# Input products of two FFNs, two feature tiles at a time, as seven half-size products

## The chip, the cores and the metric

One core of a Trainium2 chip runs the whole program. The metric is the time of one execution on the device in microseconds (us), as the median of several runs. Engines carry the profile's names: PE multiplies matrices, PEld is its weight load, DVE, ACT and POOL compute on vectors, SP issues most transfers; POOL and ACT can issue transfers too.

## The reference

Two streams of 256 tokens each, latent `x` and context `xc`, pass two layers of width 1024. A layer is FFN, token mixer, FFN; the context stream needs no second mixer output and no last FFN. What the change touches are the FFNs:

```python
def _swiglu(h, w1, w3, w2):
    return (jax.nn.silu(h @ w1) * (h @ w3)) @ w2
for l in range(DEPTH):
    x  = x  + mx[2] * 0.5 * _swiglu(_modulate(x,  norm_gain[l, 0], mx[0], mx[1]), ffn1_w1[l], ffn1_w3[l], ffn1_w2[l])
    xc = xc + mc[2] * 0.5 * _swiglu(_modulate(xc, norm_gain[l, 0], mc[0], mc[1]), ffn1_w1[l], ffn1_w3[l], ffn1_w2[l])
    ...
    x  = x  + mx[8] * 0.5 * _swiglu(_modulate(x,  norm_gain[l, 2], mx[6], mx[7]), ffn2_w1[l], ffn2_w3[l], ffn2_w2[l])
```

`h` is 512 tokens by 1024 and `w1`, `w3` are 1024 by 2816 (22 feature tiles of 128). All is float32. The vectors `mx`, `mc` come from the conditioning vector by a product with `ada_w` (nine vectors of 1024 per layer and stream).

## The kernel before, in words

Features lie on the 128 partitions, the 512 tokens on the columns: latent tokens are columns 0 to 255 (`HX`), context tokens 256 to 511 (`HC`). Every float32 product is made of three PE matmuls: an operand is cut into a high part and a rest, and `mm3` (lines 211 to 213) adds rest by high, high by rest and high by high.

- **Weights.** `unit` (line 187) loads 128x1024 weights into a buffer `raw` (four buffers, SP), ACT casts it to `whi` (line 201), DVE subtracts to get `wlo` (line 202); four buffers of each.
- **FFN** (`ffn`). The first two feature tiles are made as soon as the normed chunks `h` come (the start phase, 256 columns at a time). Each further tile takes two units, for `w1` and `w3`, and 48 matmuls of 512 columns: `silu` on ACT, the gate product `gg` on DVE (line 463), and the cut into `g`. The 22 tiles go in groups (`FF_GROUPS`); after each group `out_phase` multiplies its tiles by `w2` for the eight output chunks and adds them to `x` (line 405).
- **Conditioning.** `ada` computes those vectors on DVE: per chunk one load into `araw` (two buffers) and one 128x1024 multiply-and-sum `junk` for each stream (line 276), called a dot below. A call of `hook(n)` issues about 2n dots, after a tile (`HOOK[0]`) or an output chunk (`HOOK[1]`).
- **Order.** PE runs in the order in which the code is written; for the other engines a scheduler sets a fixed order when the program is built. Each engine executes its own in order.

Four FFNs run: layer 0's first (about 20 to 385 us), layer 0's second (936 to 1290), layer 1's first (1300 to 1650) and layer 1's second, on latent tokens alone (2020 to 2215).

## Time and profile before

| | |
|---|---|
| time of the runs | 2222.62 us median of 3 (2222.49 to 2224.86) |
| span of the profiled execution | 2221.8 us |
| PE busy | 2205.7 us (99%), 12165 matmuls |
| weight load PEld busy | 1876.2 us (84%) |
| DVE, ACT, POOL busy | 1451.5 (65%), 944.7 (43%), 95.2 us (4%) |
| moved by DMA | 312.74 MB, mean 141 GB/s |

The span reaches from the first to the last instruction; the median run is 0.8 us longer than it. A busy time is the time in which at least one instruction of that engine was in flight, so pipelined matmuls can fill it without running at their best rate.

### The profile page before, as it was taken

Reading aid. Unit: us, or ns where it says so; the run is one execution under the profiler, and the core shown is the slowest. Engines: PE = TensorE matmul, PEld = TensorE weight load, DVE = VectorE, ACT = ScalarE, POOL = GpSimd, SP = SyncE. Lnnn points to the kernel's source line nnn. Section 1 sums busy time; section 2 is a strip of 40 time slices with the busy share of each in tenths; the row PEclk is TensorE's granted clock in tenths of the full one; section 3 lists DMA queues with packets and bytes.
Section 4 is the critical chain, followed back from the end, with each engine's and each line's share of the span. In section 5 each row is a group of like instructions: output and inputs, shape, how many; then the busy total and the mean of one; then the engine's idle time right before and its main releaser. Section 6 shows DMA issues by size and latency. Waiting matters only on the chain.

```text
span 2221.8 us, 32917 instructions
## 1 busy us (share of the span) xinstructions
PE 2205.7 (99%) x12165; PEld 1876.2 (84%) x12165; DVE 1451.5 (65%) x3452; ACT 944.7 (43%) x2519; POOL 95.2 (4%) x126
## 2 busy tenths in 40 slices
...
GB/s 326 189 217 175 217 185 169 98 88 67 56 80 97 83 58 98 121 186 211 179 215 279 200 76 98 102 89 101 92 127 104 87 114 107 160 137 167 182 181 114
DMA packets 89330, 312.74 MB, mean 141 GB/s; under 512 B 10320, under 2 KB 11216, under 8 KB 89168
## 3 DMA queue, kind: packets, MB, share of 16 engines
...
## 4 chain that ended last, share of the span: by engine, by line
PE 88%; issue 9%; DVE 1%; ACT 1%; DMA 0%; POOL 0%; POOLq 0%; DVEq 0%; SPq 0%; ACTq 0%
PE mm L211 21%; PE mm L212 20%; PE mm L213 20%; PE s L212 6%; PE s L211 6%; PE s L213 6%; PE o L206 2%; PE s L206 2%; PE t L206 2%; PE t L774 1%; PE mm L206 1%; PE t L551 0%; PE s L838 0%; PE s L840 0%; PE t L789 0%
## 5 line engine op out<-in xcount | busy, mean ns | idle before, releaser
L201 ACT CAST whi<-raw 128x256 fp32r<-128x256 f32 (+2 forms) x1446 | 536.7, 433 | 561.7 <-issue 272.1
L202 DVE TENSOR_TENSOR wlo<-raw,whi 128x256 fp32r<-128x256 f32 (+1 forms) x1438 | 587.2, 455 | 269.8 <-ACT whi L201 266.2
L211 PE MATMUL mm<-h,wlo 128*128 128x512 f32 (+1 forms) x1432 | 515.0, 360 | 0.0
L213 PE MATMUL mm<-h,whi 128*128 128x512 f32 (+1 forms) x1432 | 506.0, 353 | 0.0
L212 PE MATMUL mm<-h,whi 128*128 128x512 f32 (+1 forms) x1432 | 505.8, 353 | 0.0
L211 PEld LDWEIGHTS mm<-h,wlo 128*128 128x128 f32 x1432 | 270.7, 189 | 44.8 <-issue 9.4
L213 PEld LDWEIGHTS mm<-h,whi 128*128 128x128 f32 x1432 | 270.6, 189 | 37.8
L212 PEld LDWEIGHTS mm<-h,whi 128*128 128x128 f32 x1432 | 271.0, 189 | 34.8 <-issue 0.2
L276 DVE SCALAR_TENSOR_TENSOR junk<-araw,cond 128x1024 bf16<-128x1024 f32 x224 | 271.3, 1220 | 24.0 <-DMA araw<-in_ada 23.5
L211 PE MATMUL mm<-g,wlo 128*128 128x512 f32 (+1 forms) x767 | 267.4, 349 | 0.0
L212 PE MATMUL mm<-g,whi 128*128 128x512 f32 (+1 forms) x767 | 266.5, 347 | 0.0
L213 PE MATMUL mm<-g,whi 128*128 128x512 f32 (+1 forms) x767 | 266.5, 347 | 0.0
L211 PE MATMUL s<-h,wlo 128*128 128x512 f32 (+1 forms) x688 | 246.9, 359 | 0.0
L212 PE MATMUL s<-h,whi 128*128 128x512 f32 (+1 forms) x688 | 246.9, 359 | 0.0
L213 PE MATMUL s<-h,whi 128*128 128x512 f32 (+1 forms) x688 | 246.9, 359 | 0.0
L405 DVE SCALAR_TENSOR_TENSOR x<-mm,mods,x 128x256 f32<-128x256 f32 x192 | 86.0, 479 | 116.8 <-PE mm L213 116.6
L211 PEld LDWEIGHTS mm<-g,wlo 128*128 128x128 f32 x767 | 145.3, 189 | 18.3
L212 PEld LDWEIGHTS mm<-g,whi 128*128 128x128 f32 x767 | 145.3, 189 | 18.1
L213 PEld LDWEIGHTS mm<-g,whi 128*128 128x128 f32 x767 | 145.3, 189 | 18.1
L461 ACT ACTIVATE silu<-mm 128x512 f32<-128x512 f32 (+1 forms) x88 | 47.9, 544 | 242.5 <-PE mm L213 242.5
L463 DVE TENSOR_TENSOR gg<-silu,s 128x512 f32<-128x512 f32 (+1 forms) x87 | 53.9, 619 | 147.9 <-PE s L213 132.2
L211 PEld LDWEIGHTS s<-h,wlo 128*128 128x128 f32 x688 | 130.3, 189 | 19.2
...
## 6 DMA issues: line engine op xcount, KB each, us to landing
raw<-in_w SPq DMA_DIRECT2D x170, 512.0 KB, 3.9
araw<-in_ada SPq DMA_DIRECT2D x128, 512.0 KB, 3.7
raw<-in_win SPq DMA_DIRECT2D x90, 512.0 KB, 3.3
...
raw<-in_w2a SPq DMA_DIRECT2D x32, 512.0 KB, 3.9
raw<-in_wbr SPq DMA_DIRECT2D x24, 512.0 KB, 3.4
raw<-in_ada SPq DMA_DIRECT2D x16, 512.0 KB, 9.4
raw<-in_wv SPq DMA_DIRECT2D x16, 512.0 KB, 3.6
```

Of the source, the lines that this page charges most:

```text
L201: nc.scalar.copy(hi[:, c], raw[:, c])
L202: eng.tensor_tensor(out=lo[:, c], in0=raw[:, c], in1=hi[:, c].bitcast(F32), op=ALU.subtract)
L206: self.nc.tensor.matmul(out, lhsT=lhsT, rhs=rhs, start=start, stop=stop)
L211: nc.tensor.matmul(out, lhsT=sl, rhs=mh, start=start, stop=False)
L212: nc.tensor.matmul(out, lhsT=sh, rhs=ml, start=False, stop=False)
L213: nc.tensor.matmul(out, lhsT=sh, rhs=mh, start=False, stop=stop)
L276: self.nc.vector.scalar_tensor_tensor(out=junk, in0=raw, scalar=1.0, in1=cond[s], op0=ALU.mult, op1=ALU.mult, accum_out=self.mods[l][:, s, ...
L405: nc.vector.scalar_tensor_tensor(out=self.xT[c][:, hc], in0=ps[:, hc], scalar=self.mods[l][:, s, gm, c:c + 1], in1=self.xT[c][:, hc], op0= ...
L461: nc.scalar.activation(t[:, cols], pa[:, cols], AF.Silu)
L463: nc.vector.tensor_tensor(out=gg[:, cols], in0=t[:, cols], in1=pb[:, cols], op=ALU.mult)
L774: nc.tensor.transpose(pt[:, b * 128:(b + 1) * 128], P[:, b * 128:(b + 1) * 128], self.ident)
```

## The change

For layer 0's second and layer 1's first FFN, all tiles but the first two are taken two at a time. The two tiles, the two halves of the 1024 inputs and the two token streams make a 2 by 2 block product, and seven block products (`product`: 24 matmuls of 256 columns) replace eight. `W[p, 0]` to `W[p, 3]` are the four weight blocks of pair p, from a copy of the weights in that layout; in PE's order the products of a pair take: W1 with b21; W0+W2+W3 with n2; W2+W3 with n1; W0+W2 with n3; the next pair's W0 with b11 (`begin`); W3 with n4; W0+W1+W2+W3 with b22. Results add up in the banks q1, q2, q3 and are put together by ACT and DVE. W2+W3 and W0+W2 are formed by a second, accumulating transfer that POOL issues into the loaded buffer; the other sums are DVE additions. `token_forms` makes n1 to n4 from a float32 copy (`stash`) of the normed inputs, once per FFN.

Besides: the groups become 8, 8 and 6 tiles; the dots of three vectors of layer 1 move into layer 0's first FFN (paced by 3.2 and 1.5), two vectors into layer 0's second and four into layer 1's first, there only in output phases; `cond` and the probability tiles `P` share two wide buffers.

```diff
-FF_GROUPS = ((0, 8), (8, 15), (15, 22))
+FF_GROUPS = ((0, 8), (8, 16), (16, 22))
...
+STRASSEN = ((0, 1), (1, 0))
...
-HOOK = (2.2, 0.9)
+PACE = ((3.2, 1.5), (0.0, 1.0), (0.0, 1.0))
...
         out = []
         for s in range(2):
-            t = self.qkv.tile([128, 1024], F32, tag="pair", name="cond")
+            t = self.wide("cond").rearrange("p a b -> p (a b)")
             queue.dma_start(t, self.a["cvec"][s].to_broadcast([128, 1024]))
             nc.scalar.activation(t, t, AF.Silu)
             out.append(t)
...
-    def start_norm(self, l, j, acc, s, cols, tail):
+    def start_norm(self, l, j, acc, s, cols, tail, stash=False):
         if s == 0:
             self.hn = [self.pair("h", pool=self.hp) for _ in range(KD)]
             self.hready = [0, 0]
+            self.stash = [self.pair("stash", F32) for _ in range(KD // 2)] if stash else None
 
         def apply(R):
             def one(k):
                 self.modulate(self.hn[k], self.xT[k], R, self.gs[l][:, s, j, k:k + 1],
-                              self.mods[l][:, s, 3 * j, k:k + 1], cols)
+                              self.mods[l][:, s, 3 * j, k:k + 1], cols,
+                              self.stash[k // 2][:, k % 2, cols] if stash else None)
                 self.hready[s] = k + 1
                 if k + 1 < KD:
                     self.at(self.clock["pe"] + STEP, lambda: one(k + 1))
...
         return [self.a["w13"][l, i, f, j] for f in range(2) for j in range(2)]
+
+    def token_forms(self, l, j):
+        nc = self.nc
+        M = self.mods[l]
+        X, C = M[:, 0, 3 * j, :], M[:, 1, 3 * j, :]
+        dd = self.small(8, "dshift", 1)
+        nc.vector.tensor_tensor(out=dd[:, 0:4], in0=C[:, 0:4], in1=X[:, 0:4], op=ALU.subtract)
+        nc.vector.tensor_tensor(out=dd[:, 4:8], in0=C[:, 4:8], in1=C[:, 0:4], op=ALU.subtract)
+        n2, n3, n4 = ([self.pair("tf") for _ in range(2)] for _ in range(3))
+        add = nc.vector.scalar_tensor_tensor
+        at = lambda k, cols: self.stash[k // 2][:, k % 2, cols]
+
+        def cut(out, q, cols, sign):
+            src = self.stash[q][:, :, cols]
+            hi, lo = (out[:, i, :].rearrange("p (k t) -> p k t", k=2) for i in range(2))
+            nc.scalar.activation(hi, src, AF.Copy, scale=sign)
+            add(out=lo, in0=src, scalar=sign, in1=hi.bitcast(F32), op0=ALU.mult, op1=ALU.subtract)
+
+        for q in range(2):
+            for k in (2 * q, 2 * q + 1):
+                add(out=at(k, HX), in0=at(k, HC), scalar=dd[:, k:k + 1], in1=at(k, HX), op0=ALU.add, op1=ALU.subtract)
+                add(out=at(k, HC), in0=at(k + 4, HC), scalar=dd[:, 4 + k:5 + k], in1=at(k, HC),
+                    op0=ALU.add, op1=ALU.subtract)
+                hi, lo = self.hn[k][:, 0, HC], self.hn[k][:, 1, HC]
+                nc.scalar.activation(hi, at(k, HX), AF.Copy, scale=-1.0)
+                add(out=lo, in0=at(k, HX), scalar=-1.0, in1=hi.bitcast(F32), op0=ALU.mult, op1=ALU.subtract)
+            cut(n3[q], q, HC, 1.0)
+            for k in (2 * q, 2 * q + 1):
+                add(out=at(k, HX), in0=at(k, HX), scalar=C[:, k + 4:k + 5], in1=at(k + 4, HC),
+                    op0=ALU.subtract, op1=ALU.subtract)
+            cut(n2[q], q, HX, 1.0)
+            for k in (2 * q, 2 * q + 1):
+                add(out=at(k, HX), in0=at(k, HX), scalar=X[:, k + 4:k + 5], in1=at(k + 4, HX),
+                    op0=ALU.add, op1=ALU.add)
+            cut(n4[q], q, HX, -1.0)
...
+        return {"b11": plain(0, HX), "b21": plain(4, HX), "b22": plain(4, HC), "n1": plain(0, HC),
+                "n2": form(n2), "n3": form(n3), "n4": form(n4)}
+
+    def cut_weight(self, raw):
+        nc = self.nc
+        hi, lo = (self.wp.tile([128, 1024], F32R, tag=g, name=g) for g in ("whi", "wlo"))
+        nc.scalar.copy(hi, raw)
+        nc.vector.tensor_tensor(out=lo, in0=raw, in1=hi.bitcast(F32), op=ALU.subtract)
+        return hi, lo
+
+    def block(self, src, plus=None):
+        raw = self.rawp.tile([128, 1024], F32, tag="raw", name="raw")
+        self.nc.sync.dma_start(raw, src)
+        if plus is not None:
+            self.nc.gpsimd.dma_start(raw, plus, accum_op=ALU.add)
+        return raw
+
+    def product(self, out, w, acts, start, stop):
+        hi, lo = w
+        for j in range(2):
+            o = out[:, j * SEQ:(j + 1) * SEQ]
+            c = 0.0
+            for k, (mh, ml) in enumerate(acts):
+                ws = slice(j * 512 + k * 128, j * 512 + (k + 1) * 128)
+                c += self.mm3(o, hi[:, ws], lo[:, ws], mh, ml, start and j + k == 0, k == 3, skip_group_check=True)
+            self.tick(c)
+
+    def ff_pairs(self, l, i, pairs, B):
+
+
+        nc, W = self.nc, self.a["w13p"][STRASSEN.index((l, i))]
+        add = nc.vector.tensor_tensor
+        begun = {}
+
+        def begin(p):
+            r0 = self.block(W[p, 0])
+            q1 = self.mm_bank()
+            self.product(q1, self.cut_weight(r0), B["b11"], True, False)
+            s1 = self.tmp("s1")
+            nc.scalar.copy(s1, q1)
+            begun[p] = r0, q1, s1
+
+        out = []
+        for p in pairs:
+            if p not in begun:
+                begin(p)
+            r0, q1, s1 = begun.pop(p)
+            g1, g2 = (self.pair("g") for _ in range(2))
+            r1 = self.block(W[p, 1])
+            q2, q3 = self.s_bank(), self.s_bank()
+            self.product(q2, self.cut_weight(r1), B["b21"], True, True)
+            add(out=s1, in0=s1, in1=q2, op=ALU.add)
+            self.gated(s1, g1, HX)
+            n = self.block(W[p, 2], W[p, 3])
+            wn = self.cut_weight(n)
+            add(out=r0, in0=r0, in1=n, op=ALU.add)
+            self.product(q1, self.cut_weight(r0), B["n2"], False, False)
+            sv = self.tmp("sv")
+            nc.scalar.copy(sv, q1)
+            self.product(q3, wn, B["n1"], True, False)
+            r3 = self.block(W[p, 0], W[p, 2])
+            self.product(q1, self.cut_weight(r3), B["n3"], False, False)
+            sw = self.tmp("sw")
+            nc.scalar.copy(sw, q1)
+            nc.vector.scalar_tensor_tensor(out=sw, in0=sw, scalar=-1.0, in1=q3, op0=ALU.mult, op1=ALU.subtract)
+            self.gated(sw, g2, HC)
+            if p + 1 < NFF // 2:
+                begin(p + 1)
+            r4 = self.block(W[p, 3])
+            self.product(q1, self.cut_weight(r4), B["n4"], False, True)
+            su = self.tmp("su")
+            nc.scalar.activation(su, q1, AF.Copy, scale=-1.0)
+            self.gated(su, g2, HX)
+            add(out=r1, in0=r1, in1=r0, op=ALU.add)
+            self.product(q3, self.cut_weight(r1), B["b22"], False, True)
+            add(out=sv, in0=sv, in1=q3, op=ALU.add)
+            self.gated(sv, g1, HC)
+            yield [g1, g2]
+
+    def gated(self, f, gt, cols):
+        nc = self.nc
+        u, v = f[:, 0:SEQ], f[:, SEQ:T]
+        nc.scalar.activation(u, u, AF.Silu)
+        nc.vector.tensor_tensor(out=u, in0=u, in1=v, op=ALU.mult)
+        hi, lo = gt[:, 0, cols], gt[:, 1, cols]
+        nc.scalar.copy(hi, u)
+        nc.vector.tensor_tensor(out=lo, in0=u, in1=hi.bitcast(F32), op=ALU.subtract)
 
     def ffn(self, l, i, halves, first, acc, after, pre, begun=None, each=None):
         nc, a = self.nc, self.a
...
                                       k == 0, k == KD - 1)
                     self.tick(c)
             start = [self.ff_evac(banks[2 * f], banks[2 * f + 1], cols) for f in range(2)]
-            self.hook(3)
+            if (l, i) in STRASSEN:
+                pairs = self.ff_pairs(l, i, range(1, NFF // 2), self.token_forms(l, 2 * i))
         else:
             start = begun
         h = self.hn
         for gi, (f0, f1) in enumerate(FF_GROUPS):
             gts = start
             start = []
+            if (l, i) in STRASSEN:
+                while len(gts) < f1 - f0:
+                    gts += next(pairs)
+                    self.hook(self.pace[0])
             for f in range(f0 + len(gts), f1):
                 with self.tc.issue_after(self.last_act) if gi == 0 and f < HOLD and begun is None else nullcontext():
                     wa = self.unit(a["w13"][l, i, f, 0])
                 self.run(self.gemm(pa, wa, h, cols))
                 self.run(self.gemm(pb, wb, h, cols))
                 gts.append(self.ff_evac(pa, pb, cols))
-                self.hook(HOOK[0])
+                self.hook(self.pace[0])
             ng = f1 - f0
-            w2 = a["w2a"][l, i] if gi == 0 else a["w2b"][l, i, gi - 1]
+            w2 = a["w2c"][l, i] if gi == 2 else a["w2a"][l, i, gi]
             end = gi == len(FF_GROUPS) - 1
             self.out_phase(lambda c: self.unit(w2[c], ng * 128), gts, l, gm, halves,
                            acc if end else None, after if end else None, pre if end else None, each if end else None)
             if k + 3 < KD:
                 load(k + 3)
         cond = self.cond(nc.sync)
-        self.adaq = self.ada(0, range(2, NMOD), cond)
+        self.adaq = itertools.chain(self.ada(0, range(2, NMOD), cond), self.ada(1, range(3), cond))
+        self.pace = PACE[0]
...
-            P = [self.tmp("P"), self.tmp("P")]
+            PP = self.wide("P")
+            P = [PP[:, 0, :], PP[:, 1, :]]
...
             acc2 = self.tmp("acc")
             first, pre = self.first_units(self.ff_units(l, 1))
             self.mixer(l, SEQ if last else T, nxt, spills[l], acc2,
-                       lambda *v: self.start_norm(l, 2, acc2, *v), pre)
+                       lambda *v: self.start_norm(l, 2, acc2, *v, stash=not last), pre)
             if not last:
-                self.adaq = self.ada(l + 1, range(NMOD), self.cond(nc.scalar))
+                self.adaq = self.ada(l + 1, range(3, 5), self.cond(nc.scalar))
+                self.pace = PACE[1]
             acc = self.tmp("acc")
             nxt, pre = (None, None) if last else self.first_units(self.ff_units(l + 1, 0))
             if last:
                 self.ffn(l, 1, halves, first, acc, lambda s, hc, tail: self.finish(acc, tail), lambda i: None,
                          each=self.turn_out)
             else:
-                self.ffn(l, 1, halves, first, acc, lambda *v: self.start_norm(l + 1, 0, acc, *v), pre)
+                self.ffn(l, 1, halves, first, acc, lambda *v: self.start_norm(l + 1, 0, acc, *v, stash=True), pre)
                 first = nxt
+                self.run(self.adaq)
+                self.adaq = self.ada(l + 1, range(5, NMOD), self.cond(nc.scalar))
+                self.pace = PACE[2]
```

Where instructions move, two places matter. The first is one feature tile in the middle of layer 0's first FFN on DVE, between two gate products (`gg`). Before:

```order
L463 TENSOR_TENSOR gg<-silu,s 128x512
L276 SCALAR_TENSOR_TENSOR junk,mods_106<-araw,cond 128x1024
L379 TENSOR_TENSOR g<-gg,g 128x512
L276 SCALAR_TENSOR_TENSOR junk,mods_106<-araw,cond 128x1024 x2
L202 TENSOR_TENSOR wlo<-raw,whi 128x256
L276 SCALAR_TENSOR_TENSOR junk,mods_106<-araw,cond 128x1024
L202 TENSOR_TENSOR wlo<-raw,whi 128x256 x7
L463 TENSOR_TENSOR gg<-silu,s 128x512
```

The same tile on DVE with the change:

```order
L470 TENSOR_TENSOR gg<-silu,s 128x512
L281 SCALAR_TENSOR_TENSOR junk,mods_106<-araw,cond 128x1024
L384 TENSOR_TENSOR g<-gg,g 128x512
L281 SCALAR_TENSOR_TENSOR junk,mods_106<-araw,cond 128x1024 x2
L207 TENSOR_TENSOR wlo<-raw,whi 128x256
L281 SCALAR_TENSOR_TENSOR junk,mods_106<-araw,cond 128x1024
L207 TENSOR_TENSOR wlo<-raw,whi 128x256 x3
L281 SCALAR_TENSOR_TENSOR junk,mods_106<-araw,cond 128x1024
L207 TENSOR_TENSOR wlo<-raw,whi 128x256
L281 SCALAR_TENSOR_TENSOR junk,mods_106<-araw,cond 128x1024
L207 TENSOR_TENSOR wlo<-raw,whi 128x256 x3
L470 TENSOR_TENSOR gg<-silu,s 128x512
```

Between two gate products stand six dots where four stood, spread among the eight cuts of weights.

The second is the start of layer 0's second FFN on DVE. Before, from the last normed chunks `h` on:

```order
L372 SCALAR_TENSOR_TENSOR h<-mod,mods_106,h 128x256 x2
L202 TENSOR_TENSOR wlo<-raw,whi 128x256 x8
L463 TENSOR_TENSOR gg<-silu,s 128x512 x2
L202 TENSOR_TENSOR wlo<-raw,whi 128x256
L379 TENSOR_TENSOR g<-gg,g 128x512
```

With the change, sixteen 256-wide additions (lines 497 to 505) stand between the last `h` and the gate products; from these on (`tf` are the cut forms n2 to n4, `s_8940` is the first sum of a pair) the order is:

```order
L470 TENSOR_TENSOR gg<-silu,s 128x512 x2
L522 TENSOR_TENSOR wlo<-raw,whi 128x1024
L384 TENSOR_TENSOR g<-gg,g 128x512 x2
L493 SCALAR_TENSOR_TENSOR tf<-stash,tf 128x512 x2
L522 TENSOR_TENSOR wlo<-raw,whi 128x1024
L509 SCALAR_TENSOR_TENSOR stash<-stash,mods_106 128x256 x2
L566 TENSOR_TENSOR s_8940<-s_8940,s 128x512
L522 TENSOR_TENSOR wlo<-raw,whi 128x1024
L493 SCALAR_TENSOR_TENSOR tf<-stash,tf 128x512 x3
```

The eight cuts for the next tile gave way to the token forms; the second half of n2 is the last of the three forms in the last row.

## Rows read from the trace of the kernel before

**Rows 1.** The page: busy time by engine, and the chain's shares by engine.

```profile
PE 2205.7 (99%) x12165; PEld 1876.2 (84%) x12165; DVE 1451.5 (65%) x3452; ACT 944.7 (43%) x2519; POOL 95.2 (4%) x126
...
PE 88%; issue 9%; DVE 1%; ACT 1%; DMA 0%; POOL 0%; POOLq 0%; DVEq 0%; SPq 0%; ACTq 0%
```

**Rows 2.** Windows on PE: length, busy time (matmuls), granted clock, DMA share, GB/s.

```profile
1400.00:1600.00 200.00, 200.00 (x884) 1.00 0.29 95
2050.00:2200.00 150.00, 150.00 (x1252) 1.00 0.56 177
```

**Rows 3.** Timeline of DVE, gate products one tile apart: layer 1's two FFNs.

```profile
1455.20 0.69 DVE L463 TENSOR_TENSOR gg<-silu,s 128x512 f32<-128x512 f32 x1 [3.08 <-PE s L213]
...
1466.08 0.69 DVE L463 TENSOR_TENSOR gg<-silu,s 128x512 f32<-128x512 f32 x1 [3.03 <-PE s L213]
...
2102.32 0.42 DVE L463 TENSOR_TENSOR gg<-silu,s 128x256 f32<-128x256 f32 x1 [0.74 <-PE s L213]
...
2108.08 0.42 DVE L463 TENSOR_TENSOR gg<-silu,s 128x256 f32<-128x256 f32 x1 [0.68 <-PE s L213]
```

**Rows 4.** Groups by line and form on DVE: busy us, mean ns | idle before.

```profile
L202 DVE TENSOR_TENSOR wlo<-raw,whi 128x256 fp32r<-128x256 f32 x1360 | 506.9, 422 | 219.5 <-ACT whi L201 218.2
L276 DVE SCALAR_TENSOR_TENSOR junk<-araw,cond 128x1024 bf16<-128x1024 f32 x224 | 271.3, 1220 | 24.0 <-DMA araw<-in_ada 23.5
...
L202 DVE TENSOR_TENSOR wlo<-raw,whi 128x896 fp32r<-128x896 f32 x64 | 69.6, 1089 | 34.4 <-ACT whi L201 32.3
...
L463 DVE TENSOR_TENSOR gg<-silu,s 128x512 f32<-128x512 f32 x65 | 44.6, 687 | 130.5 <-PE s L213 119.8 <-ACT silu L461 10.4
...
L364 DVE SCALAR_TENSOR_TENSOR mod<-x,gs,t 128x256 f32<-128x256 f32 x88 | 38.6, 476 | 7.8 <-PE t L206 7.1 <-DVE gs L564 0.3
...
L848 DVE SCALAR_TENSOR_TENSOR P<-P,c 128x512 f32<-128x512 f32 x16 | 11.9, 745 | 0.1
```

**Rows 5.** Timeline of DVE in the first output phase: start, length, instruction.

```profile
113.62 2.76 DVE L202 TENSOR_TENSOR wlo<-raw,whi 128x256 fp32r<-128x256 f32 x8
...
120.76 1.22 DVE L276 SCALAR_TENSOR_TENSOR junk<-araw,cond 128x1024 bf16<-128x1024 f32 x1
...
121.90 1.22 DVE L276 SCALAR_TENSOR_TENSOR junk<-araw,cond 128x1024 bf16<-128x1024 f32 x1
```

**Rows 6.** Groups by line and form on ACT.

```profile
L201 ACT CAST whi<-raw 128x256 fp32r<-128x256 f32 x1360 | 460.6, 404 | 418.3 <-issue 196.6 <-PE mm L213 152.3 <-PE s L213 59.5
L201 ACT CAST whi<-raw 128x896 fp32r<-128x896 f32 x64 | 60.2, 942 | 139.4 <-issue 75.5 <-PE mm L213 49.2 <-PE s L213 8.0
```

**Rows 7.** Windows on DVE, layer 0's first FFN: two output phases with a tile each; whole.

```profile
114.00:168.00 54.00, 45.36 (x104) 1.00 0.64 214
235.00:285.00 50.00, 41.09 (x85) 1.00 0.66 214
60.00:347.00 287.00, 234.03 (x494) 1.00 0.60 198
```

**Rows 8.** Timeline of DVE at the start of layer 0's second FFN.

```profile
944.95 0.87 DVE L364 SCALAR_TENSOR_TENSOR mod<-x,gs,t 128x256 f32<-128x256 f32 x2 [2.47 <-PE t L206]
...
952.37 2.77 DVE L202 TENSOR_TENSOR wlo<-raw,whi 128x256 fp32r<-128x256 f32 x8
960.33 1.47 DVE L463 TENSOR_TENSOR gg<-silu,s 128x512 f32<-128x512 f32 x2 [5.20 <-ACT silu L461]
```

**Rows 9.** Timeline of PE at the end of that start phase.

```profile
960.58 0.40 PE L211 MATMUL mm<-h,wlo 128*128 128x512 f32 x1
```

**Rows 10.** DMA issues: tiles, queue, count, size, median us from issue to landing.

```profile
raw<-in_w SPq DMA_DIRECT2D x170, 512.0 KB, 3.9
araw<-in_ada SPq DMA_DIRECT2D x128, 512.0 KB, 3.7
...
raw<-in_wqk SPq DMA_DIRECT2D x8, 320.0 KB, 2.9
...
x<-spill POOLq DMA_DIRECT2D x8, 256.0 KB, 4.1
```

39 lines of the change are left out of this document (25 added, 14 removed).

## The prediction

> **What bounds the kernel now.** I read the page first: PE is busy for 99% of the span, and the chain of work that ended last runs on PE for 88% and in "issue" for 9% [rows 1]. A busy PE may still run below its best rate, so the windows come next: 884 matmuls in 200 us of an FFN on 512 tokens, 1252 in 150 us of the FFN on 256, both at granted clock 1.00, 2.4 GHz [rows 2]. As a few records can be missing from a trace, I take the price of a matmul from gate products one tile apart. A tile is 48 matmuls: 10.88 us with 512 columns, so 0.2267 us each; 5.76 us with 256, so 0.1200 each [rows 3]. In both streams each matmul follows the last without a wait. So the FFNs are bound by the number of matmuls times these prices, and every other engine has slack as a mean. Whether it has slack in each stage, the windows and timelines of DVE tell, below.
>
> **Prices on DVE and ACT.** Eight cuts of 256 columns take 2.76 us, or 0.336 from start to start, where one has a mean of 0.422 [rows 4, 5]; a dot of 1024 takes 1.14 from start to start (120.76 to 121.90) and has a mean of 1.22 [rows 4, 5]. So a run of instructions costs the mean less 0.08 each: 0.61 for an addition or gate product of 512, 0.40 for a scalar-tensor form of 256, 0.66 for one of 512, 1.01 for a cut of 896 [rows 4] and, by its slope, 1.14 for a cut of 1024. On ACT a cast of 256 takes 0.404 and of 896 0.942 [rows 6], so one of 1024 about 1.05, or 0.97 in a run.
>
> **Term 1, the products.** A pair of tiles before is 96 x 0.2267 = 21.76 us; after, 7 x 24 = 168 matmuls x 0.1200 = 20.16 us. Matmul columns fall by an eighth, but the half-size matmul costs 0.53 of the whole one, so a pair gains only 1.60 us. There are ten pairs in each of two FFNs: **-32 us**. The Trainium skill ("TensorE: Matmul & The Clock Gate", section Back-to-back issue gap) gives N/2.4 + 2.5 ns for a single matmul's gap: 215.8 and 109.2 ns, hence 20.72 and 18.35 us, 2.37 per pair and -47 us in all. The rows have 226.7 and 120.0, and the measurement decides.
>
> **Term 2, the token forms at the start of the two FFNs.** Before, DVE writes the last `h` at about 952.4, PE ends the start phase at 960.58, and DVE is idle for 5.2 us before the gate products [rows 8, 9]. With the change these things happen on DVE:
> - Cuts of the first pair's blocks and the stashing of `h` come ahead of the context half's modulation, where DVE idled for 2.47 us [rows 8]; they need some 4.6 us (four cuts or additions of 1.14), so the last `h` comes about 2.1 us later, 954.5.
> - Sixteen additions of 256 x 0.40 = 6.3 us, and about 1 us of turns with ACT's casts: 961.8.
> - Two gate products 1.2, a cut 1.14, two `g` 1.2, the first halves of n3 and n2 1.3, a cut 1.14: 967.8. Then two additions 0.8, a sum 0.6, a cut 1.14, and the second halves up to n2 2.0: 972.4.
>
> PE has two products, 5.76 us, after 960.58, and is then at W0+W2+W3 with n2, at 966.3. It waits 1.5 us for the first half of n2, runs six matmuls (0.7), and waits 3.9 us for the second half. That is 5.4 us, and layer 1's first FFN starts likewise: **+11 us**. Bounds: if the first cuts fit in the idle 2.47 us the stall is 3.8 each, 7.6; if each addition takes its full 0.476 and two more turns with ACT of 0.6 are added it is 8 each, 16. Queued on DVE behind the forms are the first pair's sums, which PE needs later.
>
> **Term 3, four raw buffers and the accumulating transfer.** A pair loads five blocks, two of them with an accumulation, and r0 and r1 hold their buffers long. The buffers go round like this: the cut of r4 frees a buffer for the next n; n loads (3.9 us, the row of 512 KB on SP's queue [rows 10]), is accumulated (X us), then DVE makes r0 += n, r1 += r0, the cut of n and of r0 (four of 1.14, with a turn 4.9 us); that frees r0's buffer for the next r4, which loads in 3.9 us and is cast and cut, or waits for about 6.4 us of DVE's other work. A round is 15.5 + X us against PE's 20.16. So X up to about 4.6 costs nothing for ever; with a larger X each round runs late by the excess, less what the cut weights (four buffers) hold ahead, which is about 1.2 us at the start of each group of pairs. The groups have 3, 4 and 3 pairs, and an output phase between them restores the lead. By this, X = 5 costs nothing, 5.5 costs 3 us in all, 6 costs 12, 8 costs 39.
>
> No row shows an accumulating transfer. From below: 3.9, a plain 512 KB transfer from SP. POOL's own queue moves 256 KB in 4.1 [rows 10]; the larger size adds 1.0 per 192 KB (2.9 to 3.9 from 320 to 512 KB [rows 10]), so 256 KB more adds 1.3, and 5.4. From above: twice a plain transfer, 7.8, or twice POOL's row, 8.2, as the old content is read too. I take 5.5, nearest to POOL's row: **+3 us**, 0 to 39. The Trainium skill ("DMA: Bandwidth & Descriptors", section Anatomy of one DMA — SWDGE (gpsimd) path) has 2.0 us plus bytes/436e3 for such a queue; as an estimate that is 3.2 us for 512 KB and would make this term 0. POOL's row, 4.1 us for half of it, is longer than that.
>
> In a pair DVE has nine instructions of 1.14, three of 0.61 and eight of 0.336 = 14.8 us, ACT seven casts and the copies, about 11 us, of 20.16: no bound. SP issues five loads where there were four; the accumulation stands on POOL, which is busy for 4% [rows 1].
>
> **Term 4, dots moved into layer 0's first FFN.** Three vectors x 8 chunks x 2 streams = 48 dots x 1.14 = 55 us more on DVE. It is busy there for 234 of 287 us [rows 7], so 289 of 287: this stage turns from PE's to DVE's. By pieces: the first output phase and its tile have 45.4 of 54 us [rows 7], and 12 more dots (13.7 us) make 59.1, 5 late, 6 by adding up its instructions. The second has 41.1 of 50 [rows 7], with as many more 54.8, 4 to 5 late. A tile in between has six dots where four stood: 6.4 x 1.14 + 8 x 0.336 + 1.2 = 11.2 against 10.88, even. That is some 10 us late; the weights cut ahead absorb 2.6: **+8 us**. PE would wait there for `wlo`. From below 0 (if more of the dots slip to places with slack); from above 22: `araw` has two buffers and a load of 3.7 us [rows 10], and six dots per tile are three loads, each some 0.7 us late if it starts only when its buffer's two dots are done, another 11 to 14.
>
> **Nothing.** The dots that left layer 0's second FFN cost nothing there, since PE was the bound; the four vectors in layer 1's output phases are two dots a chunk, 5.1 us of DVE in PE's 5.44 (24 x 0.2267). Groups of 8, 8 and 6 move the same work. The wide buffers of `cond` and `P` are used at different times; if a load of `cond` came late, its dots would slip, not PE.
>
> **Sum.** 2221.8 - 32 + 11 + 3 + 8 = 2211.8 us of span; the median run is 0.8 longer, so **2212.5 us**, 10 us faster.
>
> **Rivals.**
> - *All of terms 3 and 4 hidden* (X under 5, dots in gaps): 2222.6 - 32 + 8 to 11, about 2200. For it: the means of the engines [rows 1]. Against: DVE has 53 us free for 55 us of dots there [rows 7].
> - *DVE and its `araw` waits bind the first FFN*: term 4 is 19 to 22: 2224, no change. It decides when a dot's load returns later than the two dots before it are done (2.3 us plus cuts against 3.7). For it: DVE already waits 23.5 us for `araw` [rows 4]. Against: cuts stand between the dots and cover it in part.
> - *The accumulating transfer is slow*, on the other side: PE waits for `wlo` of r4 and of r0+n in every pair after a group's first. It decides at X about 6.5, where term 3 passes the 10 us of gain; at 8 it is 39 and the time 2249, at 11 about 2290. For it: the queue's row is slow for its size. Against: only two of five blocks need it, and both are requested a pair ahead where a buffer is free.
> - *A half-size matmul costs half*, 0.1133: a pair is 19.04, term 1 is -54: 2190. All rows of the 256-column FFN speak against it.
>
> **How the numbers follow.** The forecast with its bounds (2205 to 2219) 0.48; all hidden (2196 to 2205) 0.12; DVE and `araw` (2218 to 2232) 0.18; slow transfer (2227 to 2290) 0.20; half cost 0.02. Leaving out half of the slow case and the last gives 2197 to 2246. A change under 0.2%, 4.4 us, can hardly be told from none here: faster takes the first two, the last and a little of the third, 0.62; same is most of the third, 0.15; slower the fourth and the rest of the third, 0.23.
>
> **What would show it.** Term 1: windows inside a pair at 1400 matmuls per 168 us without a wait. Term 2: PE waiting about 1.5 and 3.9 us for `tf` at each of the two starts. Term 3: the landing time of POOL's transfers into `raw`, and waits of PE for `wlo` late in each group of pairs. Term 4: PE's waits for `wlo` in the first FFN, some 8 us, after the output phases, DVE there near 100%. The prediction is wrong if PE waits at `q` banks for ACT's copies, which I hold to be done within the next product (2.88 us), or if X is over 6.5.

## The result, and the profile after

The changed kernel takes 2299.72 us (median of 4 runs, 2294.51 to 2302.39) where the kernel before takes 2222.61 in the same comparison: ratio 1.0344, 95% interval 1.0331 to 1.0356. It is 77 us slower; 10 us faster was forecast. The profiled execution has a span of 2292.6 us, 70.8 more than before.

The page of the changed kernel, the parts that answer to [rows 1] and [rows 10] and the group of the dots, as in [rows 4]:

```profile
PE 2207.6 (96%) x13578; PEld 1933.6 (84%) x13578; DVE 1621.8 (71%) x3604; ACT 1058.1 (46%) x2617; POOL 131.8 (6%) x166
...
PE 60%; DVE 16%; issue 11%; DMA 11%; ACT 2%; POOL 0%; POOLq 0%; DVEq 0%; SPq 0%; ACTq 0%
...
L281 DVE SCALAR_TENSOR_TENSOR junk<-araw,cond 128x1024 bf16<-128x1024 f32 x224 | 271.6, 1218 | 22.7 <-DMA araw<-in_ada 22.3
...
raw<-in_w13p SPq DMA_DIRECT2D x100, 512.0 KB, 3.5
raw<-in_w13p POOLq DMA_DIRECT2D x40, 512.0 KB, 6.1
```

PE is no longer busy all the time, and the chain that was PE's for 88% is PE's for 60%: DVE and DMA hold 27% of it. As many dots as before (224) take as long each, and wait for `araw` no longer than before (22.3 us; 23.5 in [rows 4]). An accumulating transfer lands 6.1 us after its issue (shortest 5.2, longest 9.7, mean 6.4). The waits of PE in the changed kernel, with sum, times and longest:

```profile
PE mm L216 <- DVE wlo L522: 28.7, 13, 5.1
PE mm L216 <- DVE wlo L207: 20.5, 13, 5.8
PE mm L216 <- ACT tf L492: 3.3, 2, 1.7
...
PE mm L217 <- DVE tf L493: 2.3, 2, 1.2
```

L522 is the cut of a weight block of a pair, L207 that of a unit in the unchanged FFNs, `tf` the token forms. For all kernels below I cut the span at DVE's first gate product after a start phase (960.33 in [rows 8]; then 1324.17 and 2032.55; after: 995.10, 1370.5 and 2102.52). So **A** holds layer 0's first FFN and mixer, **B** layer 0's second FFN, **C** layer 1's first FFN and mixer; the start phase of an FFN, up to its gate products, belongs to the part before it. What is left behind C, layer 1's last FFN, stays within 1.1 us. The median is that of all executions of a run, the parts are those of the one profiled execution. That one lies within 3 us of the median, but 5.2 us under it for the changed kernel, and above it by 3.1 for five_raw, 5.0 for dots_cuts_on_pool and 7.6 for one_ffn_early_begin. A is almost the same work in the changed kernel, no_accumulate, no_pair_dots and plain_second_load, and spreads there from 32.9 to 35.6, so 2 or 3 us in one part say little. Differences to before, in us:

| run | median | A | B | C |
|---|---|---|---|---|
| before (lengths) | 2222.6 | 960.3 | 363.8 | 708.4 |
| changed kernel | 2299.7 | +34.8 | +11.5 | +23.7 |
| dots_alone | 2255.0 | +34.6 | 0.0 | -0.2 |
| pairs_without_moved_dots | 2268.2 | +2.2 | +18.8 | +22.2 |
| no_accumulate | 2248.2 | +32.9 | -7.3 | -3.0 |
| one_ffn | 2233.0 | +2.2 | +4.4 | +0.8 |
| dots_without_loads | 2279.1 | +29.6 | +16.0 | +7.5 |
| five_raw | 2283.7 | +31.4 | +9.7 | +21.2 |
| four_loads | 2306.7 | +37.7 | +17.6 | +27.8 |
| dots_cuts_on_pool | 2255.0 | +35.7 | 0.0 | +0.8 |
| no_pair_dots | 2265.2 | +35.1 | +2.1 | +2.4 |
| dots_two_thirds | 2255.4 | +14.8 | 0.0 | +16.9 |
| one_ffn_early_begin | 2238.5 | -0.1 | +7.8 | +14.9 |
| one_ffn_five_raw | 2225.0 | 0.0 | +7.4 | -5.8 |
| plain_second_load | 2276.8 | +35.6 | +3.7 | +13.8 |
| dots_one_third | 2222.8 | -0.4 | 0.0 | -0.7 |
| one_ffn_best | 2218.6 | -0.5 | 0.0 | -4.6 |
| one_ffn_best_early | 2217.7 | 0.0 | 0.0 | -5.7 |

### The profile page after: what moved, and what is told of

Same layout as the page of the kernel before. It is cut to its first block, busy times and chain, and to the rows that moved or that the text cites. A ratio compares the mean times of both kernels' runs of the same rounds, so it can differ in the third digit from the quotient of the medians.

```text
span 2292.6 us, 36217 instructions
## 1 busy us (share of the span) xinstructions
PE 2207.6 (96%) x13578; PEld 1933.6 (84%) x13578; DVE 1621.8 (71%) x3604; ACT 1058.1 (46%) x2617; POOL 131.8 (6%) x166
## 3 DMA queue, kind: packets, MB, share of 16 engines
q8 instruction: 107, 1.75, 0.3%
## 4 chain that ended last, share of the span: by engine, by line
PE 60%; DVE 16%; issue 11%; DMA 11%; ACT 2%; POOL 0%; POOLq 0%; DVEq 0%; SPq 0%; ACTq 0%
PE mm L216 15%; PE mm L217 15%; PE mm L218 14%; DVE junk L281 7%; DMA raw<-in_w13p 5%; DMA araw<-in_ada 5%; DVE wlo L522 2%; DVE wlo L207 2%; PE s L216 2%; PE s L217 2%; PE s L218 2%; PE o L211 2%; PE s L211 2%; PE t L211 2%; PE t L912 1%
## 5 line engine op out<-in xcount | busy, mean ns | idle before, releaser
L206 ACT CAST whi<-raw 128x256 fp32r<-128x256 f32 (+1 forms) x1222 | 437.9, 421 | 391.7 <-PE mm L218 139.1
L207 DVE TENSOR_TENSOR wlo<-raw,whi 128x256 fp32r<-128x256 f32 x1214 | 481.8, 440 | 185.0 <-ACT whi L206 183.1
L216 PE MATMUL mm<-h,wlo 128*128 128x256 f32 (+2 forms) x1272 | 435.4, 342 | 0.4 <-DVE wlo L207 0.4
L218 PE MATMUL mm<-h,whi 128*128 128x256 f32 (+2 forms) x1272 | 426.3, 335 | 0.0
L217 PE MATMUL mm<-h,whi 128*128 128x256 f32 (+2 forms) x1272 | 426.0, 335 | 0.0
L281 DVE SCALAR_TENSOR_TENSOR junk<-araw,cond 128x1024 bf16<-128x1024 f32 x224 | 271.6, 1218 | 22.7 <-DMA araw<-in_ada 22.3
L216 PEld LDWEIGHTS mm<-h,wlo 128*128 128x128 f32 (+1 forms) x1272 | 241.1, 190 | 33.2 <-issue 9.4
L218 PEld LDWEIGHTS mm<-h,whi 128*128 128x128 f32 (+1 forms) x1272 | 240.9, 189 | 25.4
L217 PEld LDWEIGHTS mm<-h,whi 128*128 128x128 f32 (+1 forms) x1272 | 241.3, 190 | 22.4 <-issue 0.2
L216 PE MATMUL s<-h,wlo 128*128 128x256 f32 (+1 forms) x848 | 259.0, 305 | 0.0
L217 PE MATMUL s<-h,whi 128*128 128x256 f32 (+1 forms) x848 | 258.6, 305 | 0.0
L218 PE MATMUL s<-h,whi 128*128 128x256 f32 (+1 forms) x848 | 258.5, 305 | 0.0
L522 DVE TENSOR_TENSOR wlo<-raw,whi 128x1024 fp32r<-128x1024 f32 x140 | 170.1, 1220 | 29.0 <-ACT whi L521 29.0
L217 PEld LDWEIGHTS s<-h,whi 128*128 128x128 f32 x848 | 163.1, 192 | 6.7
L218 PEld LDWEIGHTS s<-h,whi 128*128 128x128 f32 x848 | 162.9, 192 | 6.7
```

The source lines that it names most:

```text
L206: nc.scalar.copy(hi[:, c], raw[:, c])
L207: eng.tensor_tensor(out=lo[:, c], in0=raw[:, c], in1=hi[:, c].bitcast(F32), op=ALU.subtract)
L216: nc.tensor.matmul(out, lhsT=sl, rhs=mh, start=start, stop=False, **kw)
L217: nc.tensor.matmul(out, lhsT=sh, rhs=ml, start=False, stop=False, **kw)
L218: nc.tensor.matmul(out, lhsT=sh, rhs=mh, start=False, stop=stop, **kw)
L281: self.nc.vector.scalar_tensor_tensor(out=junk, in0=raw, scalar=1.0, in1=cond[s], op0=ALU.mult, op1=ALU.mult, accum_out=self.mods[l][:, s, ...
```

## Experiments: which part costs what

**dots_alone.** The kernel before, with the dots placed as in the change:

```diff
...
-HOOK = (2.2, 0.9)
+PACE = ((3.2, 1.5), (0.0, 1.0), (0.0, 1.0))
...
-        self.adaq = self.ada(0, range(2, NMOD), cond)
+        self.adaq = itertools.chain(self.ada(0, range(2, NMOD), cond), self.ada(1, range(3), cond))
+        self.pace = PACE[0]
...
```

> The kernel before, with only the dots placed as in the change (48 more in layer 0's first FFN, paced by 3.2 and 1.5; the rest in the output phases of the next two FFNs) and no half-size products. Theory: the 35 us that layer 0's first FFN grew by come from the dots alone, which make DVE late with wlo in the output phases; then this FFN takes about 326 us from its first to its last gate product where it took 291, PE waits some 20 to 25 us for wlo there, and the time is 2222.6 + 35 = about 2257 us (2250 to 2262). Rival: the first FFN grew by other parts of the change too (groups of 8 tiles, the wide buffers of cond); then its growth here is under 20 us and the time 2223 to 2242.

Measured 2255.01 us, and the whole of it in A. The theory holds: layer 0's first FFN is long by its dots alone.

**pairs_without_moved_dots.** The changed kernel without these 48 dots:

```diff
-PACE = ((3.2, 1.5), (0.0, 1.0), (0.0, 1.0))
+PACE = ((2.2, 0.9), (0.0, 1.0), (0.0, 1.0))
...
-        self.adaq = itertools.chain(self.ada(0, range(2, NMOD), cond), self.ada(1, range(3), cond))
+        self.adaq = self.ada(0, range(2, NMOD), cond)
```

> The changed kernel without the 48 dots: the three vectors of layer 1 that they make are constants, so that part of the computation is left out, and layer 0's first FFN is paced as before. Theory: the two causes add up, so the 35 us of the first FFN go and nothing else changes: 2299.7 - 35 = 2265 us (2258 to 2270), with layer 0's second FFN at about 375 and layer 1's first at about 390 us from last normed chunk to last normed chunk, as in the changed kernel. Rival: the lateness of the first FFN is made up elsewhere or the pairs suffer from the same backlog of dots; then the time is below 2250 or above 2275.

Measured 2268.2 us, as the theory has it: A loses 32.5, C is 1.5 shorter, and B is 7 longer, which stays open. By the medians the two causes add up: 32.4 us for the dots (dots_alone) and 45.6 for the rest, 78.0 together, where the changed kernel has 77.1.

**no_accumulate.**

```diff
-        if plus is not None:
-            self.nc.gpsimd.dma_start(raw, plus, accum_op=ALU.add)
```

> The changed kernel without the accumulating transfers: the two weight sums W2+W3 and W0+W2 are left out and their first term stands in for them; loads, cuts, additions and products stay. Theory: in the pairs PE waits because the sum r0 += n on DVE waits for the accumulating transfer (6.4 us as a mean, up to 9.7), and everything behind it on DVE waits as well. Of the stalls of the two FFNs (some 69 us with the slower clock after them) about 13 are the token forms and 8 the starts of the output phases, which stay; the other 48 shrink to under 10, so the time is about 2299.7 - 40 = 2260 us (2250 to 2268). Rival: the pairs are late because four raw buffers and the dots that spill into the pairs don't allow more; then the gain is under 15 us and the time above 2285.

Measured 2248.2 us, 2 under the theory's range. B falls by 18.8 and C by 26.6: the accumulating transfers cost 45 us (by the medians the whole run falls by 51), and without them both FFNs are shorter than before the change.

**one_ffn.**

```diff
-STRASSEN = ((0, 1), (1, 0))
+STRASSEN = ((1, 0),)
...
-PACE = ((3.2, 1.5), (0.0, 1.0), (0.0, 1.0))
+PACE = ((2.2, 0.9), (2.2, 0.9), (0.0, 0.0))
...
```

> Half-size products in layer 1's first FFN alone, and all dots where they were before the change (layer 0's first FFN as before, all nine vectors of layer 1 in layer 0's second FFN), so that no dot stands in the FFN with the pairs. Theory: without dots in DVE's and SP's queues the pairs wait little: -16 for the products, +6.5 for the token forms, +4 for the starts of the output phases, 3 to 12 for the accumulating transfers: 2222.6 + 0 to 7 = 2222 to 2230 us. Rival: the pairs wait as in the changed kernel whatever else stands in the queues: layer 1's first FFN is 26 us longer than before and the time about 2248.

Measured 2233.0 us, between the two. C, where the pairs stand, is 0.8 longer than before, where the changed kernel has 23.7: without dots beside them the transfers cost little. The rest is A and B, which no pair touches here. With the old groups of tiles A is as before (one_ffn_early_begin), so in A it is the groups of 8 tiles, which the prediction put at nothing; in B it is six early dots that the change takes out (one_ffn_best).

## Experiments: layer 0's first FFN

**dots_cuts_on_pool.** dots_alone, with the cuts of `w2` in this FFN's first two output phases on POOL:

```diff
-self.out_phase(lambda c: self.unit(w2[c], ng * 128), gts, ...
+self.out_phase(lambda c: self.unit(w2[c], ng * 128, pool=(l, i) == (0, 0) and gi < 2), gts, ...
```

> The kernel before with the dots placed as in the change (2255 us), and the cuts of the w2 units of the first two output phases of layer 0's first FFN on POOL instead of DVE (8 units a phase, 1.38 us each on DVE, about 2.4 on POOL). Theory: the first FFN is long because DVE has 61 us of work in an output phase and its tile, where PE has 54.4; with 11 us less it has 50 and PE no longer waits: the first FFN grows by 0 to 10 us for 34, and the time is 2223 to 2233 us. Rival: not DVE's load but the order, in which dots stand ahead of the cuts, and the loads of araw hold it back: 2240 us or more.

Measured 2255.0 us, no change: a miss, and it does not decide between DVE's load and its order. The timelines of this kernel, first DVE, then POOL:

```profile
131.99 1.75 DVE L277 SCALAR_TENSOR_TENSOR junk<-araw,cond 128x1024 bf16<-128x1024 f32 x1 [0.51 <-DMA araw<-in_ada]
...
133.78 1.64 DVE L277 SCALAR_TENSOR_TENSOR junk<-araw,cond 128x1024 bf16<-128x1024 f32 x1
...
135.34 1.22 DVE L277 SCALAR_TENSOR_TENSOR junk<-araw,cond 128x1024 bf16<-128x1024 f32 x1
```

```profile
129.91 4.42 POOL L203 TENSOR_TENSOR wlo<-raw,whi 128x256 fp32r<-128x256 f32 x4 [5.08 <-ACT whi L202]
136.70 4.81 POOL L203 TENSOR_TENSOR wlo<-raw,whi 128x256 fp32r<-128x256 f32 x4 [2.37 <-ACT whi L202]
```

While POOL cuts (129.91 to 134.33), a dot takes 1.75 or 1.64 us; when POOL is done, 1.22. What leaves DVE comes back as slower dots: over this FFN's tiles DVE is busy for 304.7 us, 298.5 in dots_alone. The relief moved. The first output phase with its tile takes 59.9 us here (length, then busy time of PE, PEld, DVE, ACT and POOL) where it takes 71.6 in dots_alone (below), and the second 53.8 for 57.6, but the tiles elsewhere are 17 us longer together.

```profile
125.85:185.75 59.90, 57.65 (x242) 46.28 (x243) 56.53 (x109) 14.08 (x41) 20.73 (x16) 0.97 0.63 206
```

**dots_two_thirds** and **dots_one_third**: dots_alone with fewer vectors moved, and with the others partly at the old pace in the next two FFNs:

```diff
-self.ada(1, range(3), cond)   # PACE[0] = (3.2, 1.5)
+self.ada(1, range(2), cond)   # PACE[0] = (2.9, 1.3); one third: range(1), (2.55, 1.1)
```

> The kernel before with two of the three vectors moved into layer 0's first FFN (32 dots instead of 48, paced by 2.9 and 1.3), the rest where the kernel before has them. Theory: the cost is that of a DVE that is full: with 26 dots in an output phase and its tile DVE has 51 to 53 us of work for PE's 54.4, and 10.5 for 10.88 in a tile, so PE hardly waits; the first FFN grows by 0 to 8 us (34 with 48 dots) and the time is 2222 to 2231 us. Rival: each moved dot costs its share, whatever DVE has left (0.7 us a dot): 2245 us.

> The kernel before with one of the three vectors moved into layer 0's first FFN (16 dots, paced by 2.55 and 1.1), vectors 1 to 4 in layer 0's second FFN at the old pace and 5 to 8 in the output phases of layer 1's first. Theory: the cost sets in when DVE is nearly full; with 252 of 287 us of work it waits for nothing long: the first FFN grows by 0 to 3 us (14.6 with 32 dots, 34.4 with 48) and the time is 2222 to 2227 us. Rival: a cost of some 0.5 us a dot from the first dot on: 2230 us or more.

Measured in A: -0.4 us with 16 moved dots, +14.8 with 32, +34.6 with 48. The last 16 cost some 20 us, about their own 18 us on DVE; the first 16 nothing. With one third, theory and time agree (2222.79, ratio 1.0000). With two thirds the forecast of 0 to 8 fell short: DVE need not be over full. The first output phase with its tile, window by window (length, then busy time of PE, PEld, DVE, ACT and POOL), in dots_one_third, dots_two_thirds and dots_alone:

```profile
118.14:172.41 54.27, 54.27 (x241) 44.95 (x240) 46.62 (x105) 14.24 (x42) 0.00 (x0) 1.00 0.68 223
```

```profile
119.72:179.87 60.15, 56.02 (x237) 45.01 (x236) 53.09 (x122) 13.39 (x40) 0.00 (x0) 0.97 0.71 228
```

```profile
121.13:192.70 71.57, 59.34 (x230) 45.36 (x230) 61.57 (x138) 13.05 (x38) 0.00 (x0) 0.93 0.66 218
```

With 46.6 us of DVE work the stretch keeps PE's 54.3; with 53.1, still less than 54.4, it takes 60.2; with 61.6 it takes 71.6. DVE is idle for 7 and 10 us in the longer two, in which PE waits 4.0 and 12.2 us for its cuts (`wlo`): DVE waits there for products of PE (4.4 and 3.1 us), for casts (2.4 and 0.7) and for `araw` (0 and 3.2). So PE and DVE wait for each other in turn. That this comes of DVE's fixed order, with dots ahead of cuts, is argued: no run changes the order alone. That dots_two_thirds as a whole took 2255 us has another reason, in where I put the rest: the vectors 5 to 8, of one stream, stood in the tiles of layer 1's first FFN with a load for each dot, DVE waited 21.8 us there for `araw`, and a gate cast came late (its waits of PE from 1300 to 1720):

```profile
PE mm L212 <- ACT g L379: 13.1, 2, 12.1
```

## Experiments: the accumulating transfers

**dots_without_loads.**

```diff
-                nc.sync.dma_start(raw, a["ada"][l, m, k])
+                if m == mods[0] and k < 2:
+                    nc.sync.dma_start(raw, a["ada"][l, m, k])
```

> The changed kernel, with every dot in its place, but with the loads of the conditioning weights left out (but for the first two of each of the four lists of vectors): the dots read what stands in araw, so the conditioning vectors are not computed. In the runs so far the accumulating transfers cost some 45 us where dots stand in the output phases and about 4 in the FFN without dots. Theory A: it is the dots' loads: they share the DMA engines with the accumulating transfers (6.4 us as a mean and up to 9.7, where the shortest takes 5.2) and stand ahead of the weights in SP's queue; without them the pairs wait under 15 us in all, and the first FFN is shorter by the 9 us of DVE's waits for araw: 2299.7 - 30 - 9 = 2260 us (2250 to 2270). Theory B: it is the dots' own time on DVE, ahead of the sums in its order; then only the 9 us and little of the pairs' waits go: 2280 to 2292 us.

Measured 2279.1 us, and neither theory holds as a whole. C loses 16 of its 23.7 us, as A says; layer 0's first FFN loses 5; but B grows by 4.5, and why it does is not settled.

**five_raw.**

```diff
-        self.rawp = mk("rawp", 4)
+        self.rawp = mk("rawp", 5)
...
-"gg": ("c", 3, T), "PT": ("c", 3, T), "junk": ("c", 3, T)   # diag, lamj: 2
+"gg": ("c", 2, T), "PT": ("c", 2, T), "junk": ("c", 2, T)   # diag, lamj: 1
```

> The changed kernel with five raw buffers for four (to make room, the buffers shared by gg, junk and PT are two for three, and one for two small tiles of the mixer). Theory: a fifth buffer lets the loads and accumulations of a pair start about a fifth of a pair, 4 us, earlier, which covers most of what a round of four buffers is late: of the 45 us of the accumulating transfers 30 go: about 2270 us (2258 to 2280). Rival: the transfers are late since the DMA engines are full, or DVE's order holds the sums back; an earlier request changes little: above 2285 us.

Measured 2283.7 us, a little under the bound of the rival: 16 us less by the medians where 30 were expected. In the profiled executions, which lie 8 us closer together than the medians, it is 7.6, and B and C lose 4.3 of it. An earlier request takes off half of the loss at most.

**four_loads.** No accumulating transfer, four loads a pair:

```diff
-            n = self.block(W[p, 2], W[p, 3])
+            r2, r4 = self.block(W[p, 2]), self.block(W[p, 3])
+            nc.gpsimd.tensor_tensor(out=r2, in0=r2, in1=r4, op=ALU.add)
...
+            nc.gpsimd.tensor_tensor(out=r1, in0=r1, in1=r0, op=ALU.add)
+            add(out=r0, in0=r0, in1=r4, op=ALU.subtract)
```

> The changed kernel without accumulating transfers and with all of its arithmetic: a pair loads its four blocks once each; W2+W3 and W0+W1+W2+W3 are added on POOL (about 2.4 us each, by POOL's 1.83 us for 768 columns), W0+W2+W3 and W0+W2 on DVE (the second as a difference), so DVE has as much to do as before. Theory: with the accumulating transfers and three of seven transfers a pair gone, the pairs wait as little as without the sums: about 2248 us (2243 to 2257), the first FFN unchanged. Rival: the sums in a chain, POOL's ahead of DVE's, take the place of the transfers: 2262 to 2285 us.

Measured 2306.7 us, the slowest of all and beyond the rival's range. So it is not the count of transfers. SP's loads of blocks wait for buffers that DVE's cuts free, and the sum on POOL takes the place of the transfer in the same round. The waits of DVE for it in this kernel (sum, times, longest):

```profile
DVE raw L571 <- POOL raw L569: 39.6, 12, 4.5
```

**no_pair_dots.**

```diff
...
-                self.adaq = self.ada(l + 1, range(3, 5), self.cond(nc.scalar))
...
-                self.adaq = self.ada(l + 1, range(5, NMOD), self.cond(nc.scalar))
```

> The changed kernel without any dots in the two FFNs with pairs: vectors 3 to 8 of layer 1 are constants and the loads of cond and of their weights are left out, so that part of the computation is missing; layer 0's first FFN keeps its 160 dots, and the accumulating transfers stay. Theory: neither the transfers nor the dots alone make the pairs late; a round of the raw buffers is some 22 us with the transfers alone (20.16 on PE) and 27 to 34 with dots on DVE and their loads on the DMA engines. Without dots the transfers cost 3 to 6 us an FFN: the time is that without accumulating transfers, 2248, plus 6 to 12: 2253 to 2261 us. Rival: the transfers are late by themselves in layer 0's second FFN, where leaving out the dots' loads alone didn't help; then the time stays above 2270.

Measured 2265.2 us, 4 above the theory's range and 5 below the rival's. B and C are 4.5 us over before together; with dots and no accumulation 10.2 under; with both 35.2 over. So beside the dots the transfers cost 45 us; alone they stand 15 us above the run that has dots and no transfers, and 31 more come only when both are there (no run leaves out both). dots_without_loads divides the 31: with the dots on DVE but without their loads B and C are 23.6 over, so 19 come with the dots' work on DVE and 12 with their loads. The two FFNs differ in this: in B the work makes 14 and the loads -4.5, in C 5 and 16. C's dots have a load each, B's a load for two; whether that is the reason is not tested.

**plain_second_load.**

```diff
-            self.nc.gpsimd.dma_start(raw, plus, accum_op=ALU.add)
+            self.nc.gpsimd.dma_start(raw, plus)
```

> The changed kernel, where POOL's second transfer into the loaded buffer is a plain copy that overwrites it, so the two weight sums are left out (their second term stands in); it still waits for the first load and has the same bytes. Theory: accumulating keeps the DMA engines busy about twice as long as copying, and that is the larger part: the transfer lands in 4 to 4.5 us for 6.4 and the two FFNs are 20 to 30 us shorter: 2270 to 2280 us. Rival: the second step in the chain is what costs, whatever it does: above 2287 us.

Measured 2276.8 us, as the theory has it for the time; the landing is a little longer than it had (4 to 4.5), by the DMA issues of this kernel:

```profile
raw<-in_w13p POOLq DMA_DIRECT2D x40, 512.0 KB, 4.7
```

B and C are 17.5 over before, so of the 45 us about 18 belong to adding rather than copying, and 28 to a second transfer that starts when the first has landed, its bytes included. It is the adding and not POOL's queue (q0) that keeps the DMA engines longer. The same bytes take 3.7% of 16 engines' span in this kernel and 6.1% in the changed one (packets, MB, share):

```profile
q0 software_dynamic: 7808, 27.27, 3.7%
```

```profile
q0 software_dynamic: 7808, 27.27, 6.1%
```

How much longer, the DMA queues of the changed kernel from 1500 to 1550 us show (q1 has the plain transfers, most of them SP's), with its issues there:

```profile
q1 hardware_dynamic: 2662, 9.67, 57.8%
q0 software_dynamic: 575, 2.10, 22.9%
...
araw<-in_ada SPq DMA_DIRECT2D x10, 512.0 KB, 5.5
raw<-in_w13p SPq DMA_DIRECT2D x8, 512.0 KB, 4.3
raw<-in_w13p POOLq DMA_DIRECT2D x4, 512.0 KB, 8.7
```

and the same in one_ffn, whose pairs have no dots, from 1445 to 1495:

```profile
q1 hardware_dynamic: 1540, 5.60, 33.7%
q0 software_dynamic: 576, 2.10, 24.1%
...
raw<-in_w13p SPq DMA_DIRECT2D x11, 512.0 KB, 3.2
raw<-in_w13p POOLq DMA_DIRECT2D x4, 512.0 KB, 6.0
```

A plain MB takes 57.8% of 50 us for 9.67 MB, 3.0 us of all engines; an accumulated one 11.5 / 2.10 = 5.5. Pairs alone use 58% of the DMA engines; with the dots' ten loads it is 81%, and every transfer is longer: 4.3 for 3.2, 8.7 for 6.0. DVE then stands still at the sum r0 += n. Its timeline at the four pairs of layer 1's second group, in one_ffn, then in the changed kernel:

```profile
1429.90 1.23 DVE L570 TENSOR_TENSOR raw<-raw 128x1024 f32<-128x1024 f32 x1 [3.97 <-DMA raw<-in_w13p]
...
1463.47 1.23 DVE L570 TENSOR_TENSOR raw<-raw 128x1024 f32<-128x1024 f32 x1 [2.20 <-DMA raw<-in_w13p]
...
1486.10 1.23 DVE L570 TENSOR_TENSOR raw<-raw 128x1024 f32<-128x1024 f32 x1 [4.68 <-DMA raw<-in_w13p]
...
1508.28 1.23 DVE L570 TENSOR_TENSOR raw<-raw 128x1024 f32<-128x1024 f32 x1 [2.81 <-DMA raw<-in_w13p]
```

```profile
1483.56 1.22 DVE L570 TENSOR_TENSOR raw<-raw 128x1024 f32<-128x1024 f32 x1 [2.33 <-DMA raw<-in_w13p]
...
1518.06 1.23 DVE L570 TENSOR_TENSOR raw<-raw 128x1024 f32<-128x1024 f32 x1 [4.29 <-DMA raw<-in_w13p]
...
1546.69 1.23 DVE L570 TENSOR_TENSOR raw<-raw 128x1024 f32<-128x1024 f32 x1 [3.76 <-DMA raw<-in_w13p]
...
1571.10 1.23 DVE L570 TENSOR_TENSOR raw<-raw 128x1024 f32<-128x1024 f32 x1 [0.72 <-DMA raw<-in_w13p]
```

From sum to sum it is 33.6, 22.6 and 22.2 us without dots, and 34.5, 28.6 and 24.4 with them, where PE needs 20.16 for a pair. The first distance is long in both, since the first pair's sum is made while PE is still in the output phase: 15 us before the pairs begin on PE in one_ffn (1445.3), 8 us in the changed kernel (1491.3). The other two are the rounds. PE needs 85.0 us for these four pairs in one_ffn and 101.7 in the changed kernel; 4 x 20.16 is 80.6. So the round with dots is 24 to 29 us; the 34 in the expectation of no_pair_dots is that first distance.

## Experiments: a faster version

All four have half-size products in layer 1's first FFN alone, and the groups and dots of the kernel before elsewhere, but for six early dots that only the last two have.

```diff
+PLAIN_GROUPS = ((0, 8), (8, 15), (15, 22))   # for the FFNs without pairs; all four
...
+            if p == 1:                        # one_ffn_early_begin, one_ffn_best_early
+                begin(2)
...
+        self.rawp = mk("rawp", 5)             # one_ffn_five_raw, one_ffn_best, one_ffn_best_early
...
+            else:                             # one_ffn_best, one_ffn_best_early:
+                self.hook(3)                  # FFNs without pairs, at their start, as before
```

> Half-size products in layer 1's first FFN alone, the other FFNs with their groups of 8, 7 and 7 tiles and their dots as before the change, and in the first pair the next pair's product W0 by b11 ahead of the product with n2. Theory: the run with one FFN was 10 us slower, of which about 6 came from groups of 8 tiles in FFNs with dots; those go, 2226 to 2227. The product put forward gives PE 2.9 us of work while DVE makes n2, of 3.9 us of waits and the slower clock behind them: 2222 to 2225 us. Rival: the product takes a raw buffer and a PSUM bank early, and the first pair's other loads come late: 2226 to 2231 us.

Measured 2238.5 us, a miss on the rival's side and beyond it. With four raw buffers the early product makes C 14 us longer than in one_ffn in the profiled execution, the slowest of five; by the median it is nearer to 7.

> Half-size products in layer 1's first FFN alone, the other FFNs as before the change in groups and dots, and five raw buffers for four (with two buffers for three of gg, junk and PT). Theory: without the dots, a round of the raw buffers (22.2 us for 20.16 on PE) is what is left of the pairs' waits; a fifth buffer ends them: 2226.5 - 3 = 2221 to 2225 us. Rival: the round is set by DVE's order and the transfer's own time, not by the number of buffers: 2225 to 2229 us.

Measured 2225.0 us, at the edge of both: C falls to -5.8, 6.6 below one_ffn, but B, which has no pair, is 7.4 longer.

> As the run with half-size products in layer 1's first FFN alone and five raw buffers (2225.0 us), and with the six dots at the start of the other FFNs back, which the change had taken out. Theory: without them layer 0's second FFN still has dots at the start of its last output phase, where PE waited 4 us for a g that stood behind them, and the slower clock followed; with them back it takes 364 us as before the change for 371: 2225 - 6 = 2219 us (2216 to 2221). Rival: the new pool sizes or the stash of the normed inputs make that FFN longer: 2223 to 2226 us.

Measured 2218.64 us, ratio 0.9980, interval 0.9971 to 0.9989: the six early dots were the 7 us of B. C is 4.6 shorter than before, where term 1 alone has 16.

> The same with the second pair's first product ahead of the first pair's product with n2. With four raw buffers this made layer 1's first FFN longer; theory: with five the buffer that it takes early is there, and it fills 2.9 us of the wait for n2: 2215 to 2218 us, 2 to 3 below the run without it. Rival: five are still too few for it: the same or longer.

Measured 2217.65 us, ratio 0.9974, interval 0.9964 to 0.9984. It is faster than both kernels, by 5 us (0.2%) against before; the step from one_ffn_best, 1 us, is smaller than what tells the two intervals apart.

## Why the prediction was wrong

**Term 1 (-32 us) was right.** Where nothing waits, a pair takes 20.16 us: the timeline of DVE in no_accumulate, the same sum one pair later,

```profile
1034.39 0.69 DVE L577 SCALAR_TENSOR_TENSOR sw<-sw,s 128x512 f32<-128x512 f32 x1 [1.19 <-ACT sw L576]
...
1054.55 0.69 DVE L577 SCALAR_TENSOR_TENSOR sw<-sw,s 128x512 f32<-128x512 f32 x1 [1.19 <-ACT sw L576]
```

The rival that a half-size matmul costs half is out.

**Term 2 (+11 us) came out, in part by luck.** PE waits for `tf` at both starts (the rows of its waits above), but for 5.6 us in all, under the term's lower bound of 7.6. The rest is a slower clock, which the term didn't have. PE of the changed kernel, by windows:

```profile
1000.00:1004.00 4.00, 2.25 (x17) 1.00 0.53 185
1004.00:1010.00 6.00, 4.66 (x20) 0.52 0.34 107
1010.00:1014.00 4.00, 4.00 (x31) 0.86 0.11 16
```

Here are 68 matmuls in 14 us; at 0.12 they are 8.2, so 5.8 us are lost (a little less if records are missing), 2.8 of them in the waits and the rest with the clock granted at 0.52 for a stretch behind them; the other start has the like, so some 12 for the two.

**Term 3 (+3 us) failed: it measures 45** (no_accumulate), beyond its bounds (0 to 39). A part of it is X, the transfer's time. X was taken as 5.5; its median is 5.4 without dots (one_ffn), and with them 6.1 (mean 6.4), still under the 6.5 that the prediction named as a sign of being wrong. By the prediction's own rounds, which give its 12 us at 6 and 39 at 8, an X of 6.4 costs 17, less than half of the 45. (At 5.5 they give 4.6 and not 3, and they pass the gain near 6, not 6.5.) Two steps weigh more:

- *The round* was put at 15.5 + X. Without dots it is 22.2 to 22.6 with X at 5.4 to 5.6, so about 17 + X. In one_ffn's round from 1463.47 on, the block that is loaded into r0's buffer has landed at 1471.2, but ACT casts it at 1473.8, behind its casts of the gate products, which wait for DVE; and POOL issues the accumulation 0.6 us after the first load has landed. The load and the turn behind other work follow each other; they were counted as if they ran side by side. With 17 + X and X at 6.4 the same rule gives 38, an estimate.
- *The lead.* Dots and output phases were said to cost nothing and to restore it. They take it away: the dots run on into the second group's pairs, in front of the sums on DVE, and their loads fill the DMA engines; of the 45 us 31 come only beside them.

The slow transfer did stand among the rivals, with 2249 us at X = 8 and a range up to 2290. The measured time lies above this too, with X at 6.4 as a mean.

**Term 4 (+8 us) failed: it measures 34.6** (32.4 by medians). The work was counted rightly (59.1 us for the first output phase with its tile; 61.6 in dots_alone), but lateness was taken as its excess over PE's time, less a lead. In that stretch, 17 us longer than PE's 54.3, PE waits 12.2 us where 5 were forecast, by its waits in dots_alone from 121.13 to 192.70:

```profile
PE mm L212 <- DVE wlo L203: 12.2, 8, 2.8
```

The other 5 us are slower matmuls: PE is busy for 59.34 us in place of 54.27, at a mean granted clock of 0.93. The loss begins below 100% (53.1 of 54.4): DVE idles while PE waits for it. Why is argued above and not shown; the number of raw buffers is a small part of it at most, since A is still 31.4 longer with five. The rival with the `araw` waits (19 to 22) had 11 to 14 us for them; the run without the loads shows 5.

**Not in the sum: the slower clock.** The terms price work and waits, at the full clock. PE over B and C, before and in the changed kernel:

```profile
960.33:2032.55 1072.22, 1067.21 (x5821) 1.00 0.43 141
```

```profile
995.10:2102.52 1107.42, 1059.23 (x7243) 0.98 0.53 155
```

PE's busy time falls by 8 us, where the products take 32 off: 24 us of the 67 that are lost there are matmuls at a lower clock, and 43 are waits.

**Not in the sum: small waits.** B and C of no_accumulate are 10 under before, where 32 - 12 is 20. For the 10 us that are left its waits of PE show 7.8 besides those for `tf`: 2.1 for `sv`, 1.8 for `wlo`, 1.4 for `sw`, 1.7 for `g` where a group's output phase begins with a gate product just made, and 0.8 for `h`.

In all: -32 + 12 + 45 + 35 + 10 = +70, against 70.8 in the span; the 10 is what was left over, so that the sum closes is no proof of it. A part of it was in reach of the profile before: [rows 7] have DVE at 82% in layer 0's first FFN, and seven transfers a pair beside the dots' loads meet on the same DMA engines; the prediction priced each transfer by itself.
